# Layer-1 adaLN parts of a hybrid GLA/mLSTM backbone: both 512-column halves of a part summed over the partitions in one step

## The chip, the cores and the metric

The kernel runs on one core of one Trainium2 chip. The metric is the device time of one execution in microseconds (us). Before the change it is 1614.91 us, the median of three runs (1614.43 to 1615.12). One execution was also taken with the hardware profiler; the trace and all rows below are of that one.

The engines are named as the profile names them: PE is TensorE's matmul, PEld its weight load, DVE is VectorE, ACT is ScalarE, POOL is GpSimd, SP is SyncE, which issues nearly all DMAs. Each engine works through its own queue in order.

## What is computed

Two trunk layers, each a token mixer (layer 0 gated linear attention, layer 1 mLSTM) followed by a ConvFFN, over 512 latent tokens and 256 context tokens of width 1024. Each layer is modulated by adaLN: six vectors of 1024 (shift, scale and gate of mixer and FFN) come from a conditioning vector. The context stream has a conditioning vector of its own, and layer 1 needs only the first two of its parts.

```python
for i in range(DEPTH):                      # DEPTH = 2
    need_ctx = i < DEPTH - 1
    mod_l = (silu(c) @ ada_w[i] + ada_b[i])[:, None, :]
    mod_c = silu(c_ctx) @ ada_w[i] + ada_b[i]
    sh1_l, sc1_l, g1_l, sh2_l, sc2_l, g2_l = split(mod_l, 6)
    sh1_c, sc1_c, g1_c, sh2_c, sc2_c, g2_c = split(mod_c, 6)
    h_c = rmsnorm(ctx) * (1 + sc1_c) + sh1_c
    h_l = rmsnorm(x) * (1 + sc1_l) + sh1_l
    o_c, o_l = mixer(h_c, h_l)              # GLA, then mLSTM
    x = x + g1_l * o_l
    h_l = rmsnorm(x) * (1 + sc2_l) + sh2_l
    x = x + g2_l * conv_ffn(h_l)
    if need_ctx:                            # the same for ctx, with g1_c, sc2_c, sh2_c, g2_c
        ...
return rmsnorm(x) * final_g
```

## The kernel before

All activations lie transposed: 128 channels on the partitions, tokens along the row. Large projections are done in a split form: each operand is divided into a rounded high part and a low rest, and `mm3` (lines 384 to 386) issues three matmuls, high x high, high x low, low x high, in the type fp32r. Weights come by DMA into a staging tile (`load_w`, line 362), ACT writes the high part (line 340) and DVE the low part (line 341). Everything else on PE (transposes, state updates of the scans, sums over partitions) is a plain fp32 matmul.

The adaLN vectors of part p and layer l are made by the generator `ada_seq`, one step at a time. A part is 1024 columns of `ada_w`, done in two halves of 512. For each of eight blocks k of 128 input channels one step multiplies the loaded block [128, 512] with a scalar per partition: for k = 0 on ACT (line 555, it starts the accumulator `asum`), else on DVE (line 558, it adds to it). The loads (line 540) run two steps ahead with three buffers. After k = 7 the accumulator must still be summed over the 128 partitions. PE does that with a matrix of ones 32 wide (line 567): four matmuls, each writing another group of 32 partitions of one PSUM tile. ACT copies the result (line 569), the next step turns it by a PE transpose (line 572), and DVE adds the bias into `mod` (line 575 where two streams are done, line 581 where one is). The accumulators share two buffers (`bufs=2`).

With two streams there are two accumulators per half, and the four matmuls are 256 columns wide (two quarters of two accumulators); two transposes follow. With one stream alone there is one accumulator, the four matmuls are 128 wide, and one transpose follows. One stream alone holds for layer 1, parts 2 to 5. A half is ten steps: eight products, one that ends with the sums and the copy, one with the transposes and the add. Part 2 is done in the FFN of layer 0 (`project`, line 1624, one step after a projection), parts 3 to 5 in the four heads of the mLSTM scan.

In the mLSTM, a head's scan alternates with other work through a `Filler`: after each scan step it runs projection steps worth 1.6 us (`FILL1`), and whenever 1.9 us of these have passed it takes one step of the `side` generator, here 15, 19, 18 and 8 steps of `ada_seq` for the four heads. What a generator yields is its cost in us and is taken off what the filler owes. The filler's work is the value projection (tiles `vpsmv`), the gate (`mo`), the keys and queries of the next head (`mk`, `mq`) and the output projection (`po1...`). The scan itself transposes keys (`mkp`, line 1458), ACT scales them (`mktok`, line 1460), PE makes the update (`mu`, line 1465), DVE or ACT adds it to the state (`C`, lines 1469 and 1471), and later `num` (lines 1497 and 1498) gives the outputs. The framework that records the program may place instructions on their engines in another order than they are written.

Of the kernel before, what the change touches and what calls it, by code (L numbers as in the profile page):

```python
# [16 lines left out]
F32 = mybir.dt.float32  # L17
# [3 lines left out]
AF = mybir.ActivationFunctionType  # L21
ALU = mybir.AluOpType
PSUM = bass.MemoryType.PSUM

P = 128
D = 1024
KT = D // P
# [273 lines left out]
class Body:  # L301
# [226 lines left out]
    def ada_seq(self, parts):  # L528

        nc = self.nc
        steps = [(l, part, half, k) for l, part in parts for half in range(2) for k in range(KT)]

        def load(l, part, half, k):
            st = self.pw.tile([P, 512], F32, tag="ada_w", name=f"ast{l}_{part}{half}{k}", bufs=3)
            c = part * D + half * 512
            nc.sync.dma_start(st, self.a['ada_w'][l][k * P:(k + 1) * P, c:c + 512])  # L540
            return st

        ahead = [load(*x) for x in steps[:2]]
        yield 0.0
        for i, (l, part, half, k) in enumerate(steps):
            st, nm = ahead.pop(0), f"{l}_{part}{half}"
            if i + 2 < len(steps):
                ahead.append(load(*steps[i + 2]))

            both = l == 0 or part < 2  # L550
            c = [self.sil[:, k, s:s + 1] for s in range(2 if both else 1)]
            if k == 0:
                acc = [self.pw.tile([P, 512], F32, tag="ada_sum", name=f"asum{s}_{nm}", bufs=2) for s in range(len(c))]
                for s in range(len(c)):
                    nc.scalar.activation(acc[s], st, AF.Copy, scale=c[s])  # L555
            else:
                for s in range(len(c)):
                    nc.vector.scalar_tensor_tensor(acc[s], st, c[s], acc[s], op0=ALU.mult, op1=ALU.add)  # L558
            yield 0.0
            if k < KT - 1:  # L560
                continue

            ps = self.ada_tile(f"ada{nm}")
            n = 256 if both else 128
            for j in range(4):
                x = acc[j % 2][:, j // 2 * n:j // 2 * n + n] if both else acc[0][:, j * n:j * n + n]
                nc.tensor.matmul(ps[32 * j:32 * j + 32, 0:n], self.ones, x, start=True, stop=True)
            ev = self.pw.tile([P, 256], F32, tag="adaev", name=f"aev{nm}", bufs=1)
            nc.scalar.copy(ev[:, :n], ps[:, :n])
            yield n / 474  # L570
            for i_ in range(n // P):
                nc.tensor.transpose(ps[:, 256 + i_ * P:256 + (i_ + 1) * P], ev[:, i_ * P:(i_ + 1) * P], self.ident)
            b = part * KT + half * 4
            if both:
                nc.vector.tensor_tensor(
                    self.mod[l][:, b:b + 4, :].rearrange("p (q i) s -> p q i s", i=2),
                    ps[:, 256:512].rearrange("p (i q s x) -> p q i s x", i=2, q=2, x=32)[:, :, :, :, 0],
                    self.adab[l][:, b:b + 4].rearrange("p (q i) -> p q i", i=2).unsqueeze(3).to_broadcast([P, 2, 2, 2]),
                    op=ALU.add)
            else:  # L580
                nc.vector.tensor_tensor(self.mod[l][:, b:b + 4, 0], ps[:, 256:384:32], self.adab[l][:, b:b + 4], op=ALU.add)
            if half and part in (1, 4):
                self.make_A(l, part // 4, 0, KT, 2 if both else 1)
            yield n / 1164

    def ada_step(self, n=1):
        for _ in range(n):
# [1247 lines left out]
```

## Time and profile before

| | us |
|---|---|
| median of three runs (lowest, highest) | 1614.91 (1614.43, 1615.12) |
| the profiled execution | 1615.44 |
| its span, first to last instruction | 1613.4 |
| PE busy | 1594.7 (99%) |
| DVE busy | 1231.5 (76%) |
| ACT busy | 678.9 (42%) |

A matmul's printed duration runs to its modelled end, and the next one starts before that; so the spacing of starts, and not the duration, says how long a matmul holds the queue. A wait is idle time of an engine, put down to the instruction that came last before it ended. Records of line 567 come in twos: each fp32 matmul there stands as two records, so four matmuls are "x8".

### The profile page before, as it was taken

The numbers are of one execution on the slowest core, as the hardware profiler recorded it, in microseconds if no ns is written. First come the engines' busy times: TensorE is split into PE (matmuls) and PEld (weight loads), VectorE is DVE, ScalarE is ACT, GpSimd is POOL, SyncE is SP. The second block draws the span as 40 slices with busy tenths as digits, with TensorE's granted clock in tenths as the row PEclk, the third lists the DMA queues.
The fourth block names the chain that finished last, engine by engine and source line by source line (L and its number), as shares of the span: only waits on it lengthen the run. The fifth ranks groups of instructions, "written<-read, shape, count | busy, mean of one in ns | idle before, by whom it ended". The sixth has DMA issues, their size and how long they took to land. (4 is left out here: it accounts for less than half of the span.)

```text
span 1613.4 us, 23563 instructions
## 1 busy us (share of the span) xinstructions
PE 1594.7 (99%) x9249; PEld 1379.1 (85%) x9249; DVE 1231.5 (76%) x2123; ACT 678.9 (42%) x1149; POOL 68.6 (4%) x128
## 2 busy tenths in 40 slices
PE   7999999999999999999999999999999999999998
PEld 6789898888888888888888988888889888888887
DVE  5866978878985978686755778766778988877875
ACT  5683738435431314131322356545465422323334
POOL 0010101011000000000000020000001000000000
PEclk9999999999999999999999999999999999999999
DMA  8613453432240524251312204433330423223321
GB/s 303 190 47 107 125 152 92 141 89 88 83 124 27 147 76 118 66 169 50 102 53 63 57 27 150 134 119 102 98 118 14 129 89 97 85 81 98 117 79 53
DMA packets 178674, 163.59 MB, mean 101 GB/s; under 512 B 8924, under 2 KB 146788, under 8 KB 178564
## 3 DMA queue, kind: packets, MB, share of 16 engines
q1 hardware_dynamic: 178324, 161.97, 33.4%
q8 instruction: 72, 1.18, 0.3%
q14 instruction: 38, 0.31, 0.1%
q10 hardware_dynamic: 240, 0.13, 0.0%
HBM read 159.98 MB, written 2.10 MB: 100 GB/s over the span
## 5 line engine op out<-in xcount | busy, mean ns | idle before, releaser
L1648 DVE SCALAR_TENSOR_TENSOR acc<-gp,vt_f,acc 128x512 f32<-128x512 f32 x352 | 260.2, 747 | 4.6
L558 DVE SCALAR_TENSOR_TENSOR asum<-ast,sil,asum 128x512 f32<-128x512 f32 x224 | 163.7, 753 | 21.3 <-ACT asum L555 11.3
L384 PE MATMUL fd<-ahil,wh_d 128*128 128x512 f32 (+1 forms) x376 | 142.0, 378 | 0.3 <-DVE xl L629 0.2
L386 PE MATMUL fd<-ahil,wl_d 128*128 128x512 f32 (+1 forms) x376 | 141.7, 378 | 0.0
L385 PE MATMUL fd<-alol,wh_d 128*128 128x512 f32 (+1 forms) x376 | 141.4, 376 | 0.0
L629 DVE SCALAR_TENSOR_TENSOR xl<-fd,mod,xl 128x512 f32<-128x512 f32 (+1 forms) x128 | 90.7, 714 | 55.7 <-PE fd L386 55.4
L384 PE MATMUL fa<-hhi,wh_a 128*128 128x512 f32 x320 | 124.9, 390 | 0.0
L384 PE MATMUL fg<-hhi,wh_g 128*128 128x512 f32 x320 | 124.8, 390 | 0.0
L385 PE MATMUL fg<-hlo,wh_g 128*128 128x512 f32 x320 | 124.6, 389 | 0.0
L386 PE MATMUL fg<-hhi,wl_g 128*128 128x512 f32 x320 | 124.6, 389 | 0.0
L386 PE MATMUL fa<-hhi,wl_a 128*128 128x512 f32 x320 | 124.6, 389 | 0.0
L385 PE MATMUL fa<-hlo,wh_a 128*128 128x512 f32 x320 | 124.5, 389 | 0.0
L1649 ACT ACTIVATE acc<-acc,vt_f 128x256 f32<-128x256 f32 (+1 forms) x66 | 43.1, 653 | 173.1 <-DVE acc L1648 172.9
L340 ACT CAST wh_a<-st_a 128x1024 fp32r<-128x1024 f32 x43 | 45.2, 1052 | 102.3 <-PE fg L385 86.3
L1632 ACT COPY gp<-fg 128x512 f32<-128x512 f32 x40 | 23.3, 582 | 146.1 <-PE fg L386 146.1
L384 PEld LDWEIGHTS fd<-ahil,wh_d 128*128 128x128 f32 x376 | 70.7, 188 | 13.6 <-DVE xl L629 1.1
L386 PEld LDWEIGHTS fd<-ahil,wl_d 128*128 128x128 f32 x376 | 70.6, 188 | 13.0 <-DVE wl_d L341 0.2
L385 PEld LDWEIGHTS fd<-alol,wh_d 128*128 128x128 f32 x376 | 70.7, 188 | 12.4
L341 DVE TENSOR_TENSOR wl_a<-st_a,wh_a 128x1024 fp32r<-128x1024 f32 x43 | 52.5, 1220 | 33.7 <-ACT wh_a L340 33.7
L340 ACT CAST wh_d<-st_d 128x1024 fp32r<-128x1024 f32 x44 | 45.9, 1050 | 75.9 <-PE fd L385 54.2
L386 PEld LDWEIGHTS fa<-hhi,wl_a 128*128 128x128 f32 x320 | 60.1, 188 | 12.6
L386 PEld LDWEIGHTS fg<-hhi,wl_g 128*128 128x128 f32 x320 | 60.1, 188 | 12.6
(1436 smaller groups left out, 4483.0 us busy)
## 6 DMA issues: line engine op xcount, KB each, us to landing
ast<-in_ada_w_dram SPq DMA_DIRECT2D x160, 256.0 KB
st_g<-in_ffn_w_up_dram SPq DMA_DIRECT2D x44, 512.0 KB
st_a<-in_ffn_w_up_dram SPq DMA_DIRECT2D x44, 512.0 KB
st_d<-in_ffn_w_down_dram SPq DMA_DIRECT2D x44, 512.0 KB
ast<-in_ada_w_dram SPq DMA_DIRECT2D x16, 512.0 KB
st_wo<-in_gla_w_out_dram SPq DMA_DIRECT2D x14, 512.0 KB
st_gr<-in_gla_w_in_dram SPq DMA_DIRECT2D x8, 512.0 KB
st_mo<-in_mlstm_w_in_dram SPq DMA_DIRECT2D x8, 512.0 KB
```

The source lines that it names most:

```text
L340: return (nc.scalar.copy(hi, src), (eng or nc.vector).tensor_tensor(lo, src, hi.bitcast(F32), op=ALU.subtract))
L341: (eng or nc.vector).tensor_tensor(lo, src, hi.bitcast(F32), op=ALU.subtract))
L384: nc.tensor.matmul(ps, wl[0], wr[0], start=start, stop=False)
L385: nc.tensor.matmul(ps, wl[0], wr[1], start=False, stop=False)
L386: nc.tensor.matmul(ps, wl[1], wr[0], start=False, stop=stop)
L558: nc.vector.scalar_tensor_tensor(acc[s], st, c[s], acc[s], op0=ALU.mult, op1=ALU.add)
L629: self.nc.vector.scalar_tensor_tensor(xv, ps, gate, xv, op0=ALU.mult, op1=ALU.add)
L1632: nc.scalar.copy(g[:, 1:ROWS + 1, 1:W_GRID + 1], ps[c0].rearrange("p (r w) -> p r w", r=ROWS))
L1648: nc.vector.scalar_tensor_tensor(o, s, tw, o, op0=ALU.mult, op1=ALU.add)
L1649: nc.scalar.activation(acc[:, c0:c0 + n], acc[:, c0:c0 + n], AF.Gelu_apprx_tanh, bias=cb[:, c:c + 1])
```

## The change

In layer 1, parts 2 to 5, the first half now keeps its accumulator and goes through two empty steps in place of the sums and of the transpose. The second half gets another accumulator, and after its last product four matmuls of 256 columns sum both (two quarters of each accumulator), one copy of 256 columns follows, then two transposes and one add for all eight blocks of the part. The number of steps stays ten per half; the costs that they yield are 0 and 0 for a first half, 0.54 and 0.22 for a second half (before 0.27 and 0.11 for each). Parts with two streams do the same as before, with the same order of matmuls.

```diff
             if k == 0:
-                acc = [self.pw.tile([P, 512], F32, tag="ada_sum", name=f"asum{s}_{nm}", bufs=2) for s in range(len(c))]
+                new = [self.pw.tile([P, 512], F32, tag="ada_sum", name=f"asum{s}_{nm}", bufs=2) for s in range(len(c))]
                 for s in range(len(c)):
-                    nc.scalar.activation(acc[s], st, AF.Copy, scale=c[s])
+                    nc.scalar.activation(new[s], st, AF.Copy, scale=c[s])
+                acc = new if both or not half else acc + new
             else:
                 for s in range(len(c)):
-                    nc.vector.scalar_tensor_tensor(acc[s], st, c[s], acc[s], op0=ALU.mult, op1=ALU.add)
+                    nc.vector.scalar_tensor_tensor(acc[s - len(c)], st, c[s], acc[s - len(c)], op0=ALU.mult, op1=ALU.add)
             yield 0.0
             if k < KT - 1:
                 continue
+            if not (both or half):
+
+                yield 0.0
+                yield 0.0
+                continue
 
             ps = self.ada_tile(f"ada{nm}")
-            n = 256 if both else 128
             for j in range(4):
-                x = acc[j % 2][:, j // 2 * n:j // 2 * n + n] if both else acc[0][:, j * n:j * n + n]
-                nc.tensor.matmul(ps[32 * j:32 * j + 32, 0:n], self.ones, x, start=True, stop=True)
+                q, i_ = (j // 2, j % 2) if both else (j % 2, j // 2)
+                nc.tensor.matmul(ps[32 * j:32 * j + 32, 0:256], self.ones, acc[i_][:, q * 256:q * 256 + 256],
+                                 start=True, stop=True)
             ev = self.pw.tile([P, 256], F32, tag="adaev", name=f"aev{nm}", bufs=1)
-            nc.scalar.copy(ev[:, :n], ps[:, :n])
-            yield n / 474
-            for i_ in range(n // P):
+            nc.scalar.copy(ev, ps[:, :256])
+            yield 0.54
+            for i_ in range(2):
                 nc.tensor.transpose(ps[:, 256 + i_ * P:256 + (i_ + 1) * P], ev[:, i_ * P:(i_ + 1) * P], self.ident)
...
             else:
-                nc.vector.tensor_tensor(self.mod[l][:, b:b + 4, 0], ps[:, 256:384:32], self.adab[l][:, b:b + 4], op=ALU.add)
+                b = part * KT
+                nc.vector.tensor_tensor(
+                    self.mod[l][:, b:b + KT, 0].rearrange("p (q i) -> p q i", i=2),
+                    ps[:, 256:512].rearrange("p (i q x) -> p q i x", i=2, x=32)[:, :, :, 0],
+                    self.adab[l][:, b:b + KT].rearrange("p (q i) -> p q i", i=2), op=ALU.add)
...
-            yield n / 1164
+            yield 0.22
```

In the changed code the products are lines 555 and 559, the sums line 572, the copy line 575, the transposes line 578; everything behind is ten lines further on.

PE in the FFN of layer 0, at the first half of part 2 (`fg` is the gate projection, `ada_20` the PSUM tile of part 2, half 0). Before:

```order
L386 MATMUL fg_7394<-hhi_3904,wl_g_7385 128x512
L567 MATMUL ada_20_7419<-asum_1_20_6924,ones 32x128 x4
L384 MATMUL fg_7426<-chi_3906,wh_g_7384 128x256
L385 MATMUL fg_7426<-clo_3907,wh_g_7384 128x256
L386 MATMUL fg_7426<-chi_3906,wl_g_7385 128x256
```

The changed kernel at the same place:

```order
L386 MATMUL fg_7394<-hhi_3904,wl_g_7385 128x512
L384 MATMUL fg_7419<-chi_3906,wh_g_7384 128x256
L385 MATMUL fg_7419<-clo_3907,wh_g_7384 128x256
L386 MATMUL fg_7419<-chi_3906,wl_g_7385 128x256
L384 MATMUL fg_7419<-chi_3906,wh_g_7384 128x256
```

The four matmuls of 128 columns are gone from here; at the second half of part 2, 386 rows further on, the changed kernel has these:

```order
L385 MATMUL fa_7954<-hlo_3905,wh_a_7881 128x512
L386 MATMUL fa_7954<-hhi_3904,wl_a_7882 128x512
L572 MATMUL ada_21_7979<-asum_1_20_6924,ones 32x256 x2
L572 MATMUL ada_21_7979<-asum_1_21_7488,ones 32x256 x2
L384 MATMUL fa_7986<-chi_3906,wh_a_7881 128x256
L385 MATMUL fa_7986<-clo_3907,wh_a_7881 128x256
```

Both accumulators, of half 0 (`asum_1_20`) and of half 1 (`asum_1_21`), are read at that one place.

ACT at the first product of part 4 (`asum_1_40`; `aev_30` and `aev_31` are the copies of part 3, `mktok` scaled keys of the scan). Before, in the first head of the mLSTM:

```order
L1460 ACTIVATE mktok_9715<-mkp_9713,mcol 128x128
L895 COPY mvt_9461<-vpsmv_9694 128x256
L340 CAST wh_mk_9876<-st_mk_9874 128x1024
L1460 ACTIVATE mktok_9747<-mkp_9745,mcol 128x128
L569 COPY aev_30_9764<-ada_30_9759 128x128
L555 ACTIVATE asum_1_40_10277<-ast_400_10142,sil 128x512
L1460 ACTIVATE mktok_9771<-mkp_9769,mcol 128x128
L340 CAST wh_mq_10000<-st_mq_9998 128x1024
```

The changed kernel, in the second head:

```order
L1470 ACTIVATE mktok_10167<-mkp_10165,mcol 128x128
L1455 ACTIVATE Wt_10088<-Wt_10088 128x512
L1479 COPY C_10171<-mu_10169 128x257
L905 COPY mvt_10047<-vpsmv_10149 128x256
L555 ACTIVATE asum_1_40_10261<-ast_400_10125,sil 128x512
L575 COPY aev_31_10191<-ada_31_10186 128x256
L1470 ACTIVATE mktok_10195<-mkp_10193,mcol 128x128
L1470 ACTIVATE mktok_10219<-mkp_10217,mcol 128x128
L905 COPY mvt_10047<-vpsmv_10201 128x256
```

The product of part 4 has moved from the first head's scan to the second's. It stands in front of the copy of part 3, where before it stood behind that of part 3's first half.

SP from the second part of a head's value weights (`st_mv`) on, in the mLSTM. Before:

```order
L362 DMA st_mv_10072<-in_mlstm_w_in_dram 128x4x256
L540 DMA ast_403_10307<-in_ada_w_dram 128x512
L540 DMA ast_404_10337<-in_ada_w_dram 128x512
L540 DMA ast_405_10382<-in_ada_w_dram 128x512
L540 DMA ast_406_10402<-in_ada_w_dram 128x512
L540 DMA ast_407_10425<-in_ada_w_dram 128x512
L362 DMA st_mo_10368<-in_mlstm_w_in_dram 128x8x128
L540 DMA ast_410_10455<-in_ada_w_dram 128x512
```

The changed kernel:

```order
L362 DMA st_mv_10055<-in_mlstm_w_in_dram 128x4x256
L362 DMA st_mo_10352<-in_mlstm_w_in_dram 128x8x128
L362 DMA st_mo_10413<-in_mlstm_w_in_dram 128x8x128
L362 DMA st_wo_10490<-in_mlstm_w_out_dram 128x1024
L362 DMA st_wo_10496<-in_mlstm_w_out_dram 128x1024
L540 DMA ast_403_10291<-in_ada_w_dram 128x512
```

The loads of part 4 (`ast_403` and on) now stand behind the weights `st_mo` and `st_wo`; before, five of them stood ahead of the first `st_mo`. Between the last `st_wo` and the next head's key weights (`st_mk`) there are eleven loads of `ada_w` now, and eight before.

## Rows read from the trace of the kernel before

**Rows 1.** The page: the span, and busy time (share, instructions) of PE and DVE.

```profile
span 1613.4 us, 23563 instructions
...
PE 1594.7 (99%) x9249; PEld 1379.1 (85%) x9249; DVE 1231.5 (76%) x2123; ACT 678.9 (42%) x1149; POOL 68.6 (4%) x128
```

**Rows 2.** Busy time by engine from 1050 to 1100 us, then granted clock, DMA share, GB/s.

```profile
1050.00:1100.00 50.00, 50.00 (x295) 43.21 (x294) 33.98 (x75) 21.33 (x45) 0.74 (x2) 1.00 0.42 127
```

**Rows 3.** Waits of PE, 940 to 1232 us: total, times, longest.

```profile
PE wib L1425 <- DVE mstk L1339: 0.9, 1, 0.9
PE vpsmv L386 <- POOL hlo L341: 0.3, 1, 0.3
PE po134A L384 <- DVE xl L629: 0.3, 1, 0.3
```

**Rows 4.** Groups of tile ada, 760 to 1230 us: duration ns min/median/max, first and last start.

```profile
L567 PE MATMUL ada<-asum,ones x64: 272/284/298, 767.5 to 1213.0; 128*32 128x128 f32 x64
L569 ACT COPY aev<-ada x8: 243/265/273, 768.0 to 1213.3; 128x128 f32<-128x128 f32 x8
...
L572 PE MATMUL ada<-ident,aev x8: 270/271/272, 770.8 to 1217.8; 128*128 128x128 f32 x8
L581 DVE TENSOR_TENSOR mod<-ada,vt_v x8: 151/155/165, 771.2 to 1219.3; 128x4 f32<-128x4 f32 x8
```

**Rows 5.** Timeline of PE at part 2, first half: start, duration, instruction.

```profile
767.14 0.39 PE L386 MATMUL fg<-hhi,wl_g 128*128 128x512 f32 x1
767.46 0.43 PE L567 MATMUL ada<-asum,ones 128*32 128x128 f32 x8
767.81 0.39 PE L384 MATMUL fg<-chi,wh_g 128*128 128x256 f32 x1
768.04 0.28 PE L385 MATMUL fg<-clo,wh_g 128*128 128x256 f32 x1
```

**Rows 6.** Timeline of PE at a half with two streams (layer 1, part 0).

```profile
521.03 0.39 PE L386 MATMUL fg<-hhi,wl_g 128*128 128x512 f32 x1
...
522.39 0.39 PE L386 MATMUL fg<-hhi,wl_g 128*128 128x512 f32 x1
522.71 0.64 PE L567 MATMUL ada<-asum,ones 128*32 128x256 f32 x8
523.28 0.39 PE L384 MATMUL fg<-chi,wh_g 128*128 128x256 f32 x1
523.51 0.28 PE L385 MATMUL fg<-clo,wh_g 128*128 128x256 f32 x1
```

**Rows 7.** Timeline of PE at the transposes: two together, then one.

```profile
526.12 0.28 PE L386 MATMUL fg<-chi,wl_g 128*128 128x256 f32 x1
526.24 0.38 PE L572 MATMUL ada<-ident,aev 128*128 128x128 f32 x2
526.38 0.47 PE L384 MATMUL fa<-hhi,wh_a 128*128 128x512 f32 x1
526.69 0.39 PE L385 MATMUL fa<-hlo,wh_a 128*128 128x512 f32 x1
...
770.65 0.28 PE L386 MATMUL fg<-chi,wl_g 128*128 128x256 f32 x1
770.78 0.27 PE L572 MATMUL ada<-ident,aev 128*128 128x128 f32 x1
770.80 0.48 PE L384 MATMUL fa<-hhi,wh_a 128*128 128x512 f32 x1
771.12 0.40 PE L385 MATMUL fa<-hlo,wh_a 128*128 128x512 f32 x1
```

**Rows 8.** Waits of ACT, whole span: line 555 on the sums.

```profile
ACT asum L555 <- PE ada L567: 5.8, 4, 1.7
```

**Rows 9.** SP's queue at the key weights of head 2; tile wh_mk's first use.

```profile
1067.16 0.38 SPq L362 DMA_DIRECT2D st_mk<-in_mlstm_w_in_dram  x1
...
L384 PE MATMUL mk<-hhi,wh_mk x8: 389/389/395, 1099.6 to 1104.4; 128*128 128x512 f32 x8
```

More of the change, by code (lines that the diff above doesn't have):

```diff
@@ L561, in ada_seq @@
                 continue
+            if not (both or half):
+                yield 0.0
+                yield 0.0
+                continue
             ps = self.ada_tile(f"ada{nm}")
-            n = 256 if both else 128
             for j in range(4):
-                x = acc[j % 2][:, j // 2 * n:j // 2 * n + n] if both else acc[0][:, j * n:j * n + n]
-                nc.tensor.matmul(ps[32 * j:32 * j + 32, 0:n], self.ones, x, start=True, stop=True)
+                q, i_ = (j // 2, j % 2) if both else (j % 2, j // 2)
+                nc.tensor.matmul(ps[32 * j:32 * j + 32, 0:256], self.ones, acc[i_][:, q * 256:q * 256 + 256],
+                                 start=True, stop=True)
             ev = self.pw.tile([P, 256], F32, tag="adaev", name=f"aev{nm}", bufs=1)
-            nc.scalar.copy(ev[:, :n], ps[:, :n])
-            yield n / 474
-            for i_ in range(n // P):
+            nc.scalar.copy(ev, ps[:, :256])
+            yield 0.54
+            for i_ in range(2):
                 nc.tensor.transpose(ps[:, 256 + i_ * P:256 + (i_ + 1) * P], ev[:, i_ * P:(i_ + 1) * P], self.ident)
-            b = part * KT + half * 4
             if both:
+                b = part * KT + half * 4
                 nc.vector.tensor_tensor(
```

## The prediction

> **What bounds the kernel now.** I read the page first. TensorE (PE) is busy 1594.7 us of a span of 1613.4 us, VectorE 1231.5 us [rows 1]. The stretch 1050 to 1100 shows PE busy for all of its 50 us at a granted clock of 1.00, the upper of its two levels (2.4 GHz), with VectorE at 33.98 us and ScalarE at 21.33 us [rows 2]. So a microsecond that leaves TensorE's queue leaves the span, and work that leaves VectorE or ScalarE buys nothing by itself. Next I asked who PE waits for between 940 and 1232, where the change moves other work: three waits only, 0.9, 0.3 and 0.3 us [rows 3]; hardly a stall is left to be removed. Then I asked which instructions the changed lines own in layer 1: 64 records of the sums over partitions, 8 transposes, 8 copies on ScalarE and 8 adds on VectorE [rows 4]. These are eight halves, for parts 2 to 5 with two halves each.
>
> The sum uses spacing rather than the durations printed for matmuls, because these overlap. From 521.03 to 522.39 there are six steps of 512-column matmuls, 1.36 us: 0.227 each [rows 6]. A step of 256 columns is 0.12, from 526.12 to 526.24 [rows 7]. What an insertion costs is the time from the start of the matmul ahead of it to the start of the second one behind it, less those two steps. The second one is taken because the first one behind an insertion is itself stretched: in both groups, its successor starts 0.23 us after it instead of 0.12 [rows 5, 6].
>
> **The change part by part.** *The sum over partitions.* Now a half is four matmuls of 128 columns (eight records). From 767.14 to 768.04 is 0.90 us; without it 0.227 + 0.12 = 0.347, so it costs 0.55 us [rows 5]. After the change a part is four matmuls of 256 columns. The same program already runs these for the parts with two streams: from 522.39 to 523.51 is 1.12 us, less 0.347 is 0.77 us [rows 6]. Twice the columns cost 0.22 us more, not twice as much. Each part saves 2 x 0.55 - 0.77 = 0.33 us.
>
> *The transposes.* Their number stays 8, but two come together. One alone: 770.65 to 771.12 is 0.47, less 0.347, so 0.12. Two together: 526.12 to 526.69 is 0.57, less 0.347, so 0.22 [rows 7]. A part saves 2 x 0.12 - 0.22 = 0.02 us.
>
> *Together:* 4 x (0.33 + 0.02) = 1.40 us of PE's queue. Bounds: some of the halves stand next to other plain-fp32 matmuls, where the stretch on both sides may be paid anyway. If it always is, only the time from the group's start to the next start counts: 0.35 for 128 columns [rows 5], 0.57 for 256 [rows 6], so 4 x (2 x 0.35 - 0.57 + 0.02) = 0.6 us. At the other end, if a group of the first half takes all its cost away and the second half's becomes no dearer: 4 x (0.55 + 0.12) = 2.7 us. I take 1.40, since both shapes were measured in the same surroundings (a 512-column matmul ahead and 256-column ones behind), where neither bound holds.
>
> The Trainium skill, page "TensorEngine Tiling (Array Packing)", section "Instruction Overhead", says that each matmul carries an overhead of about 60 cycles. By that alone the 16 matmuls that go away would be worth, as an estimate at 2.4 GHz, 16 x 25 ns = 0.4 us, and the time would be 1614.5. The trace disagrees: the group of four with 128 columns costs 0.55 us and that with 256 columns 0.77, so more than 60 cycles per matmul is fixed.
>
> *Copies and adds.* ScalarE loses eight copies of 0.265 us and gets four of 256 columns; VectorE loses four of eight adds of 0.155 us [rows 4]. Costed at nothing: VectorE has 16 us free in 50 and ScalarE 28 [rows 2]. If that cover were gone it would still be a gain.
>
> *The accumulators live longer.* Two buffers hold the sums of a stream, and both are now kept until the second half's matmuls have read them. So the first product of the next part (line 555, ScalarE) must wait for those matmuls. This comes up at two places, part 3 to 4 and part 4 to 5; between parts 2 and 3 lies the rest of the FFN of layer 0. By the order, ScalarE has the product of part 4 in front of the copy of part 3, with the products `mktok` of the scan behind both; a late `mktok` would make PE wait at its `mu`. The trace has this same wait where both streams fill both buffers (layer 0): four times, 5.8 us together, 1.7 at the longest [rows 8]. I take nothing: PE's first `mkp` behind the wait stands itself behind the matmuls that end it, and twelve to fifteen value matmuls of 0.12 us (1.4 to 1.8 us) lie between it and the `mu` that needs it. Upper bound: 1.7 us at each of the two places, 3.4 us.
>
> *Moved accumulation.* Seven VectorE products of part 4's first half (and of part 5's) now come one scan later; they need 7 x 0.75 us there, inside the 16 us that VectorE has free [rows 2]. Nothing reads parts 3 to 5 before the norm and the FFN that follow the mLSTM, and the last matmuls of each part stay where they were.
>
> *DMA queue.* On SyncE the loads of `ada_w` that follow a held buffer now come behind the weights of `mo` and `wo`, and the key weights of the next head stand behind eleven such loads instead of eight. Now that load is issued at 1067.16 and PE's first use of it is at 1099.6 [rows 9], 32 us later; three more loads, each paced by a 0.75 us product and what lies between, do not use that up. Cost 0.
>
> *Filler.* The two yields of a first half now count 0, those of a second half 0.54 and 0.22. The total stays, but around a first half some three to six projection matmuls move across a step of the scan. No matmul is added by this; its cost is nothing or a short stall, bounded by the 0.9 us that is PE's longest wait in that stretch [rows 3].
>
> **The sum.** The profiled execution took 1615.44 us (span 1613.4 plus 2.0 around it), 0.5 above the median of 1614.91. The saving does not depend on that offset, so I take it off the median: 1614.91 - 1.40 = 1613.5 us.
>
> **The rivals.** *Slower: the held accumulators.* ScalarE stands at line 555 until PE has done the part's sums, the scan's products come late, and PE waits for them. Price up to 2 x 1.7 us [rows 8]: 1613.5 + 3.4 = 1616.9. It turns slower than before as soon as more than 0.7 us reaches PE at each place. For it: ScalarE works in order, and the order puts that product ahead. Against it: in the whole stretch PE waits for VectorE and GpSimd and never for ScalarE [rows 3]. Chance 0.20, which includes other short stalls from the moved steps; 0.06 that it passes 0.2%.
>
> *Faster than said: the moved steps close gaps.* If the 0.6 us of the last two waits go [rows 3] the result is 1612.9, and with the upper bound of 2.7 us 1612.2. Against it: little is there to be closed. Chance 0.09, of which 0.05 beyond 0.2%.
>
> *The change does not do what it says: the cost goes by columns.* The columns are the same before and after, so 1614.9; with the lower bound 1614.3. Against it: the two shapes measured above. Chance 0.09, the page's rule of 60 cycles with its 1614.5 among it.
>
> **How the numbers follow.** Forecast 0.62, at 1613.5. The range runs from 1612.2 (upper bound of the saving) to 1616.0 (most of the slower rival); about 0.15 is left out. A difference of 0.2%, 3.2 us, is about what a measurement of this kernel can tell from no change. The whole forecast and nearly all of the rivals lie inside it: faster 0.05, same 0.89, slower 0.06.
>
> **What would show it.** In the changed profile the sum line has 32 records fewer in layer 1, all of 256 columns; the group of part 2's second half (near 834) costs 0.77 us by spacing, and the place near 767 shows 512-column and 256-column matmuls without a break. Wrong would be: a wait of PE for `mktok` or `C` from ScalarE behind either of the two groups in heads 1 and 2 of the mLSTM; a wait of PE for the weights of `mk` or `mq`; or a group of 256 columns that costs 1.1 us, which would make the saving nothing.

## The result and the profile after

The changed kernel takes 1617.92 us (median of 20 runs), the kernel before 1614.82 in the same comparison (20 runs): a ratio of 1.0020, 95% interval 1.0015 to 1.0026. It is slower by 3.1 us; the forecast was 1613.5, the range ended at 1616.0. One disturbed execution each of the changed kernel, of its third run and of the run with early loads is left out of all ratios and ranges given here; without it their medians are 1617.79, 1616.78 and 1615.16.

In the profiled execution (1621.78 us) the page shows the saving and the loss side by side. This is its span and the engines' busy time, which answers [rows 1]; line numbers have moved (sums now L572, copy L575, transposes L578, adds L588, `hps` L849, `mkp` L1468, `mktok` L1470, `C` L1481):

```profile
span 1620.0 us, 23500 instructions
...
PE 1597.1 (99%) x9217; PEld 1381.0 (85%) x9217; DVE 1231.7 (76%) x2119; ACT 675.5 (42%) x1143; POOL 68.1 (4%) x128
```

PE has 32 records fewer, as said, and yet it is counted busy longer. The groups of tile `ada` from 760 to 1230 us answer [rows 4] (duration ns min/median/max, first and last start):

```profile
L572 PE MATMUL ada<-asum,ones x32: 379/391/404, 834.0 to 1219.3; 128*32 128x256 f32 x32
L578 PE MATMUL ada<-ident,aev x8: 270/271/273, 837.6 to 1224.4; 128*128 128x128 f32 x8
```

PE's waits from 940 to 1232 us (total, times, longest), against [rows 3]:

```profile
PE hps L849 <- ACT mktok L1470: 2.4, 1, 2.4
PE mkp L1468 <- DVE C L1481: 1.7, 1, 1.7
PE wib L1435 <- DVE mstk L1349: 1.0, 1, 1.0
PE vpsmv L386 <- POOL hlo L341: 0.3, 1, 0.3
```

The first two are new; a wait of PE for `mktok` behind the sums is what the prediction had named as a sign of its being wrong. They stand at 1140 and at 1068, in the two heads of the scan in which a held accumulator comes free. Behind each of them stands something that the kernel before shows in no such place. Busy time by engine, then the granted clock, DMA share and GB/s, ahead of the first wait, in it, behind it, and behind the second (against [rows 2]):

```profile
1064.00:1068.00 4.00, 4.00 (x32) 3.80 (x31) 1.53 (x4) 3.49 (x6) 0.00 (x0) 1.00 0.61 188
1068.00:1070.00 2.00, 0.51 (x3) 0.07 (x1) 2.00 (x3) 0.00 (x1) 0.00 (x0) 1.00 0.50 144
1071.50:1074.50 3.00, 3.00 (x8) 2.32 (x8) 2.57 (x5) 0.66 (x2) 0.00 (x0) 0.50 0.55 163
1143.00:1146.00 3.00, 2.96 (x10) 2.47 (x11) 1.81 (x3) 2.12 (x4) 0.00 (x0) 0.50 0.83 241
```

PE is busy behind the waits, but at its lower level, 1.2 GHz; the trace's record of the granted clock gives this level for 3.4 us each time. That is why PE's busy time grew. The matmuls show it in their spacing (timeline of PE: start, duration):

```profile
1070.25 0.33 PE L1468 MATMUL mkp<-ident,kT 128*128 128x128 f32 x1 [1.74 <-DVE C L1481]
...
1072.13 0.63 PE L384 MATMUL mo<-hhi,wh_mo 128*128 128x512 f32 x1
1072.55 0.63 PE L385 MATMUL mo<-hlo,wh_mo 128*128 128x512 f32 x1
...
1075.53 0.39 PE L386 MATMUL mo<-hhi,wl_mo 128*128 128x512 f32 x1
1075.76 0.39 PE L384 MATMUL mo<-hhi,wh_mo 128*128 128x512 f32 x1
```

A step of 512 columns takes 0.42 to 0.43 us there and 0.23 at the end: 3.4 us at half clock cost 1.7. The account of the span closes with that. By the spacing of starts the two waits cost 1.9 and 2.6 us, the two stretches at half clock 2 x 1.7, and 1.4 is taken as saved, as forecast: 1.9 + 2.6 + 3.4 - 1.4 = 6.5; the span grew by 1620.0 - 1613.4 = 6.6. This execution is one of the slowest. The kernel's runs spread from 1615.95 to 1621.78 (the kernel before: 1613.78 to 1616.20), and in three traces the waits and the half clock differ. The half clock is not needed for the loss: in the trace of the second run of the changed kernel (1617.88 us, next to the median) the waits are 1.3 and 1.9 us, no half clock stands behind them, PE is busy 1594.0, and the span is still 1615.9 - 1613.4 = 2.5 us longer.

**What is late.** First products of a half (line 555) on ScalarE stood at 1012.0, 1055.2, 1085.6 and 1128.1 in the trace of before, for the halves of parts 4 and 5: 30 to 43 us apart (ScalarE's timeline: start, duration, instruction):

```profile
1012.02 0.73 ACT L555 ACTIVATE asum<-ast,sil 128x512 f32<-128x512 f32 x1
...
1055.19 0.72 ACT L555 ACTIVATE asum<-ast,sil 128x512 f32<-128x512 f32 x1
...
1085.57 0.72 ACT L555 ACTIVATE asum<-ast,sil 128x512 f32<-128x512 f32 x1
...
1128.10 0.71 ACT L555 ACTIVATE asum<-ast,sil 128x512 f32<-128x512 f32 x1
```

Here is the same for the changed kernel (in brackets the idle time ahead and its releaser):

```profile
1054.73 0.72 ACT L555 ACTIVATE asum<-ast,sil 128x512 f32<-128x512 f32 x1 [0.19 <-PE ada L572]
...
1064.30 0.72 ACT L555 ACTIVATE asum<-ast,sil 128x512 f32<-128x512 f32 x1 [0.91 <-DMA ast<-in_ada_w_dram]
...
1130.51 0.72 ACT L555 ACTIVATE asum<-ast,sil 128x512 f32<-128x512 f32 x1 [2.41 <-PE ada L572]
...
1141.74 0.72 ACT L555 ACTIVATE asum<-ast,sil 128x512 f32<-128x512 f32 x1 [2.62 <-DMA ast<-in_ada_w_dram]
1142.37 0.35 ACT L905 COPY mvt<-vpsmv 128x256 f32<-128x256 f32 x1
1142.62 0.37 ACT L1470 ACTIVATE mktok<-mkp,mcol 128x128 f32<-128x128 f32 x1
```

The accumulators are held until 1054, so the first half of part 4 no longer runs at 1012 but at 1055, and the second half follows 10 us behind it, where there are 43 between these two in the kernel before. Part 5's halves go the same way, 1130.5 and 1141.7 in place of 1085.6 and 1128.1. Sixteen products with their loads now come in a row. SP issues the loads as fast as three buffers come free, and no faster (SP's queue; answers [rows 9]):

```profile
1055.48 13.53 SPq L540 DMA_DIRECT2D ast<-in_ada_w_dram  x11
1069.83 0.38 SPq L362 DMA_DIRECT2D st_mk<-in_mlstm_w_in_dram  x1
```

Eleven loads in 13.5 us, one each 1.2 us. The program however places the products among the scan's steps as if the loads were there. At 1141.74 ScalarE has stood 2.62 us for one load, and the next `mktok` comes behind it; PE's `hps` needs the PSUM buffer that this `mktok` reads. Near 1068 it is VectorE that stands, ahead of two products of the second half, with `wl_mo` (1.22 us) and the state update behind them, for which PE's `mkp` waits:

```profile
1067.12 1.54 DVE L559 SCALAR_TENSOR_TENSOR asum<-ast,sil,asum 128x512 f32<-128x512 f32 x2 [2.00 <-ACT mktok L1470]
```

The profile puts these 2.00 us down to `mktok`, which happened to end just then; the product does not read it. In the trace's semaphore events the load's last event stands at 1067.03, 0.09 us ahead of the product. The same 0.09 us lies between the two in the second and third execution of the changed kernel (1066.37 to 1066.46, 1065.27 to 1065.37). So it is the load that VectorE waited for.

### The profile page after: what moved, and what is told of

Same layout as the page of the kernel before. It is cut to its first block, busy times and chain, and to the rows that moved or that the text cites. A ratio compares the mean times of both kernels' runs of the same rounds, so it can differ in the third digit from the quotient of the medians.

```text
span 1620.0 us, 23500 instructions
## 1 busy us (share of the span) xinstructions
PE 1597.1 (99%) x9217; PEld 1381.0 (85%) x9217; DVE 1231.7 (76%) x2119; ACT 675.5 (42%) x1143; POOL 68.1 (4%) x128
```

## Experiments

Ratios are to the kernel before in the same comparison, with 95% intervals. Theory A is what was just told: loads that come late and in a bunch make ScalarE and VectorE stand in front of the scan's work. B is that the moved yields of the filler do it, C that the wide sums do.

**Accumulators of their own.** Part 4 gets two accumulators in a tile that is idle then, so nothing is held; the control makes the same edit to the kernel before.

```diff
...
+                if l == 1 and part == 4:
+                    if not half:
+                        self.ada_x = self.pc.tile([P, 4, 512], F32, tag="xc", name="ada_x", bufs=1)
+                    new = [self.ada_x[:, half, :]]
...
```

> The changed kernel, but part 4 of layer 1 gets accumulators of its own (a tile that lies idle in the mLSTM), so that its first product waits for no sums of part 3, and part 5 uses the buffers that part 3 has left. Theory A (the held accumulators push the next part's loads and products together behind the sums, and products that wait for a late load block ScalarE and VectorE ahead of the scan's own work): the two stalls of PE near 1068 and 1140 us go, with the two stretches at half clock behind them, and the saving of the merged sums is left: about 1613.4 us. Theory B (the moved filler steps, that is the yields of 0 and of 0.54 and 0.22, put the stalls there): the yields are the same, so about 1618. Theory C (the wider sums, copy and add themselves hold PE up): about 1618.

> The kernel before, with the same separate accumulators for part 4: it had no hold to lose, so theories A, B and C all expect 1614.8 us, within 0.7. If it is faster by over 1 us, the separate buffers do something else than theory A says.

The first took 1616.41, ratio 1.0009 (1.0001 to 1.0018), the control 1618.86, ratio 1.0022 (1.0013 to 1.0031). The first is what A wants in part: the wait at 1140 is gone. But that at 1068 stays with 1.2 us and a new one of 1.1 us (`wic`, 1046) comes up, so its 1616.41 fits neither A's 1613.4 nor the 1618 of B and C. The control was not neutral: all theories expected 1614.8. Without the wait for a buffer the framework placed part 4's products further ahead, in front of the work that starts a head's scan: waits of 1.7 and 0.6 us from 1046 on, with 3.4 us of half clock behind them. VectorE did not wait there, it was busy with these products. So a held accumulator is not the only way to bring such a wait about; a product that stands too early in an in-order queue does it as well. For the same reason the pair does not isolate what holding costs.

**The moved yields alone**, in the kernel before:

```diff
-            yield n / 474
+            yield 0.54 if both else 0.54 * half
...
-            yield n / 1164
+            yield 0.22 if both else 0.22 * half
```

> The kernel before, each half summed by itself, but with the yields of the change (0 and 0 for a first half, 0.54 and 0.22 for a second one, in the parts with one stream). Theory A: the filler's steps move, nothing is held: 1614.8 us within 0.7, no PE wait above 1 us between 1010 and 1230. Theory B: the stalls come with the moved steps: about 1618 to 1619.

1615.56, ratio 1.0003 (0.9994 to 1.0012), and no wait of PE beyond those of [rows 3] and one of 0.2. B falls as the cause of the 3 us. It may hold a small part of them: by the starts of the same matmuls this trace loses 0.6 us between 1125 and 1165.

**The change for part 2 alone**, where no other part waits for its accumulators. The other parts keep the old code:

```diff
-                acc = new if both or not half else acc + new
+                acc = new if both or not half or part != 2 else acc + new
...
-            if not (both or half):
+            if not (both or half) and part == 2:
...
+            n = 256 if both or part == 2 else 128
```

> The change for part 2 alone (in the FFN, where no scan runs beside it); parts 3 to 5 as before. Theory A and B: no stall, a quarter of the saving: 1614.5 us (0.35 below before), and by spacing the merged group at the second half of part 2 costs 0.77 us while the one near 767 is gone. Theory C (the wider sums hold PE up): a stall of PE at that group, 1615.5 or more.

1614.65, ratio 0.9998 (0.9989 to 1.0007). The time alone can't tell 0.35 from nothing. The trace can: the start of the same matmul, against the trace of before, is 0.19 us earlier from 400 to 750 and 0.54 earlier from 850 to 900, a gain of 0.35. The price of the sums was right, and the wide sums brought no wait at this place.

**Held accumulators, narrow sums.** The changed kernel, its sums at the end of the second half as eight of 128 columns:

```diff
-            for j in range(4):
+            for j in range(4 if both else 8):
...
+                i_, q = j // 4, j % 4
+                nc.tensor.matmul(ps[32 * q:32 * q + 32, i_ * P:i_ * P + P], self.ones, acc[i_][:, q * P:q * P + P],
...
```

> The changed kernel with everything moved as the change moves it (both halves' accumulators held, two empty steps, one copy, two transposes and one addition at the end of the second half), but the sums themselves as in the kernel before: eight of 128 columns instead of four of 256. The before kernel ran at 1615.1 in the last comparison, the changed one at 1617.9. Theory A (the late first load of a half stands in front of the scan's work on ScalarE and VectorE, because the first product of a half waits for the sums that free its accumulator): the two long waits of TensorE near 1068 and 1140 are there again, with the half clock behind them, and the time is the changed kernel's plus the saving that is undone, four times 0.35: 1618 to 1620. Theory C (the wider sums themselves bring the loss): no long waits, 1614.5 to 1615.5.

1615.29, ratio 1.0004 (0.9995 to 1.0013): neither A's number nor its two long waits. This looked like C. But the framework had also placed six VectorE instructions otherwise: an accumulation of `asum` stood ahead of the scan's update of `C` behind the sums, where the changed kernel has it behind. Two kernels took these two differences apart, beside the changed kernel itself. One has wide sums in the sequence 2, 3, 0, 1, which gives VectorE nearly the order of the narrow run. The other writes each wide sum as two narrow ones, which leaves VectorE's and ScalarE's orders as they are in the changed kernel.

```diff
-            for j in range(4):
+            for j in (range(4) if both else (2, 3, 0, 1)):
```

```diff
+                w = P if not both and j < 4 else 256
+                for o in range(0, 256, w):
+                    nc.tensor.matmul(ps[32 * j:32 * j + 32, o:o + w], self.ones, acc[i_][:, q * 256 + o:q * 256 + o + w],
...
```

> The changed kernel with the four sums of a part issued in another order, those of the second half's accumulator first. Instructions, widths, loads and held accumulators are the same; what differs is where the framework puts six of VectorE's instructions in the mLSTM: an accumulation now stands ahead of the scan's state update behind the sums, as in the run with held accumulators and narrow sums, instead of behind it. Theory D (the loss is decided by that order: the accumulations pace the loads, and with the state updates ahead of them the loads come later than the places at which ScalarE and VectorE are told to wait for them): the waits of TensorE near 1068 and 1140 go and the time is 1614.5 to 1615.5, about 2.5 below the changed kernel. Theory C (wide sums together with held accumulators bring the loss, whatever the order): the waits stay, 1617.5 to 1618.5.

> The changed kernel with each wide sum of a one-stream part written as two of 128 columns, eight instructions in place of four; VectorE's and ScalarE's orders stay those of the changed kernel, word for word. Theory D (the order decides): the waits of TensorE near 1068 and 1140 are there and the time is that of the changed kernel, 1617 to 1619. Theory C (the wide sums do it): no long waits, 1614.5 to 1615.5, as in the run with held accumulators and narrow sums. For the price of the sums: if what a group costs goes by its columns plus one fixed part for each interruption of the projection, these eight cost the 0.77 of four wide ones; if each instruction has its fixed part, 1.1.

> The changed kernel itself once more, on the same chip as the three others of this batch, so that they can be compared with it and not with the kernel before alone. Every theory expects 1617 to 1618.5, with the two long waits of TensorE near 1068 and 1140 in most executions.

They took 1617.54 (ratio 1.0020, 1.0011 to 1.0029), 1617.87 (1.0019, 1.0010 to 1.0028) and 1618.14 (1.0023, 1.0013 to 1.0034). So C falls, narrow sums are as slow as wide ones; but the order of those six instructions does not decide alone either. The narrow run was then repeated beside the changed kernel on one chip:

> The run with held accumulators and narrow sums once more, now beside the changed kernel on one chip. Theory D (small differences in VectorE's order decide whether the late loads reach TensorE): 1615 to 1616 again, at least 1.5 below the changed kernel, no wait of TensorE over 0.8 near 1068 and none near 1140. Theory G (the difference was the chip's): 1617 to 1618.5 like the changed kernel, with the two waits.

> The changed kernel on the same chip as the three others. Theory D: 1617 to 1618.5 again. Theory G: what the run with narrow sums gives, within 0.7.

1615.97 (1.0005, 0.9996 to 1.0014) and 1616.78 (1.0015, 1.0006 to 1.0024): 0.8 us apart, less than the 1.5 expected, and with intervals that overlap; nor was the wait near 1140 gone, as expected. Neither of the two theories of these runs holds. What all these kernels have in common is seen in PE's waits between 1040 and 1160, first the repeated narrow run, then the narrow sums in the changed kernel's order, then the changed kernel's second and third run:

```profile
PE hps L851 <- ACT mktok L1472: 1.0, 1, 1.0
PE mkp L1470 <- DVE C L1483: 0.3, 1, 0.3
```

```profile
PE hps L851 <- ACT mktok L1472: 1.8, 2, 1.5
PE mkp L1470 <- DVE C L1483: 1.4, 1, 1.4
```

```profile
PE hps L849 <- ACT mktok L1470: 1.9, 1, 1.9
PE mkp L1468 <- DVE C L1481: 1.3, 1, 1.3
```

```profile
PE hps L849 <- ACT mktok L1470: 2.1, 1, 2.1
PE mkp L1468 <- DVE C L1481: 1.7, 1, 1.7
```

They are the same two waits in all, of different length. With the sequence 2, 3, 0, 1 they are 1.1 and 1.1, in the first narrow run 0.2 and 0.9. Wherever the accumulators of parts 3 and 4 are held, ScalarE stands for loads between 1040 and 1150, 2.2 to 3.6 us in all. In the changed kernel's first trace:

```profile
ACT asum L555 <- DMA ast<-in_ada_w_dram: 3.5, 2, 2.6
```

The kernel before and the version with parts 2 and 5 alone have no such wait there. But what decides how much of it reaches PE is not shown: the run with the sequence 2, 3, 0, 1 has 2.2 us of it and takes 1617.54, the repeated narrow run has 2.6 and takes 1615.97. VectorE's waits for loads as a sum tell even less; the kernel before has more of them than the changed one's 3.6 in the same stretch, and PE feels none:

```profile
DVE asum L558 <- DMA ast<-in_ada_w_dram: 4.0, 7, 1.4
```

So it must be the place of a wait, ahead of work that PE needs next; this is argued from the chains told here. One of them is seen on VectorE in the second run of the changed kernel, in front of the state update:

```profile
1066.46 1.54 DVE L559 SCALAR_TENSOR_TENSOR asum<-ast,sil,asum 128x512 f32<-128x512 f32 x2 [1.53 <-DMA ast<-in_ada_w_dram]
1067.92 1.22 DVE L341 TENSOR_TENSOR wl_mo<-st_mo,wh_mo 128x1024 fp32r<-128x1024 f32 x1
1069.05 0.48 DVE L1481 SCALAR_TENSOR_TENSOR C<-C,dec,mu 128x257 f32<-128x257 f32 x1
```

**Loads issued earlier.** The changed kernel with four more load buffers and a look-ahead of six steps for most of parts 3 to 5:

```diff
...
-            if i + 2 < len(steps):
-                ahead.append(load(*steps[i + 2]))
+            while at < min(len(steps), i + (7 if deep and 12 <= i < 36 else 3)):
+                ahead.append(load(*steps[at]))
+                at += 1
...
```

> The changed kernel with four more load buffers for parts 3 to 5, in a tile that is idle at that time, and loads issued six steps ahead instead of two; the accumulators are held as in the changed kernel. Theory A in its form that the loads come late (bunched behind the sums, the products wait for them): neither ScalarE nor VectorE waits for a load near 1068 and 1140, the long waits of TensorE and the half clock go, and the time is 1613 to 1614.5, below both kernels. Rival K (the wait for the accumulator alone does it, whenever the loads come): the waits stay, 1617 to 1618.5. Rival L (earlier loads collide with the weights' loads on SP's queue): a wait for a weight tile appears near 1050 to 1150, 1615 to 1618.

1615.64, ratio 1.0002 (0.9993 to 1.0011). The accumulators are held as long as in the changed kernel, and the two long waits are gone: PE's longest behind 1040 is 0.3 us, VectorE's for loads fell from 3.6 us to 1.2 between 1040 and 1150. Rival K falls with that: an accumulator can be held and the two waits be gone. The wait for a weight tile that rival L expects is 0.2 us, on ScalarE. But the framework moved the products as well, ScalarE's first ones of the second halves from 1064.3 and 1141.7 to 1059.2 and 1132.6, and VectorE's order differs. So the run does not tell earlier loads from this other order. It does not reach the 1613 to 1614.5 that was expected. One first product, whose load goes through an old buffer, still stands 3.1 us on ScalarE; no long wait of PE follows, but by the starts of the same matmuls some 1.1 us, the sums' own cost taken out, is lost between 1125 and 1160 in small pieces.

**The first product on GpSimd** in place of ScalarE:

```diff
-                    nc.scalar.activation(new[s], st, AF.Copy, scale=c[s])
+                    if both:
+                        nc.scalar.activation(new[s], st, AF.Copy, scale=c[s])
+                    else:
+                        nc.gpsimd.tensor_scalar(new[s], st, c[s], None, op0=ALU.mult)
```

> The changed kernel with the first product of each one-stream half on GpSimd instead of ScalarE; loads, accumulators and sums stay. Theory A, for the wait near 1140 (ScalarE stands at that product 2.6 us for its load, in front of the copies on which the scan waits): ScalarE's wait for the load and TensorE's wait of 2.4 us there go, with the half clock behind it (1.7): 1613.4 to 1616, at least 2 below the changed kernel's 1617.9; the wait near 1068, in which VectorE stands in front of the scan's state, may stay. Rival H (it is VectorE's accumulations, which wait for the same loads, that hold the scan at both places): both waits stay and the time is 1617 to 1619.

1622.59, ratio 1.0047 (1.0034 to 1.0059; five runs), the slowest of all and outside what either theory gave. At the place for which it was made it did what A says: ScalarE waits for no load there, and PE's wait for `mktok` is gone, with 1.2 us for VectorE's `C` in its place. But the product is slower on GpSimd (1.58 us median against 0.72), and one at 986.8 came after a wait of 1.8 for its load and took 2.54. The framework had also placed four accumulations ahead of `mstk`, with which the first head starts; two of them stood 1.2 and 1.6 us for loads on VectorE, and `mstk` came late, at 996.7 (994.4 in the changed kernel). PE's waits, 940 to 1232:

```profile
PE wib L1438 <- DVE mstk L1352: 3.7, 1, 3.7
PE mkp L1471 <- DVE C L1484: 1.9, 1, 1.9
PE hps L852 <- DVE C L1484: 1.2, 1, 1.2
```

**A wait made on purpose.** The kernel before, with ten (then twenty) copies on VectorE ahead of one state update of head 1:

```diff
+                for _ in range(10 if (h, d, s) == (1, 1, 2) else 0):
+                    nc.vector.tensor_copy(C[d][nx], C[d][p])
```

> The kernel before with ten copies of 128 x 257 on VectorE (each bounded by the 0.48 us of the state's update) ahead of one update of the state in the second head's scan; the copies write what the update then overwrites, so nothing else changes, neither loads nor sums. It measures what a wait of TensorE costs here. Theory M (a wait of about 2 us is followed by 3.4 us of half clock, which costs another 1.7): one wait of TensorE of 1 to 4 us on VectorE near 1065 to 1080, half clock behind it, and a time above the kernel before by that wait plus about 1.7: 1618 to 1620. Rival N (the half clock in the changed kernel has another cause): the wait alone, clock at full level, 1616 to 1618.

> The kernel before with twenty copies of 0.33 us on VectorE ahead of one state update in the second head's scan, 6.6 us in place of the 3.3 that left no wait of TensorE. About half should reach TensorE: a wait of 1.5 to 4 us near 1065 to 1075. Theory M (a wait of about 2 us can be followed by 3.4 us of half clock): in most executions 1.7 us more than the wait, 1618 to 1620, and a spread of 3 us or more between executions. Rival N (the half clock has another cause): the wait alone and the spread of the kernel before, 2.5 us.

1614.65 (ratio 1.0001, 0.9992 to 1.0009) and 1616.14 (1.0005, 0.9996 to 1.0013). Ten copies, some 3 us of VectorE, brought no wait of PE beyond [rows 3]; twenty brought one of 0.5 us. The question that they were made for, what the half clock adds to a wait of 2 us, they could not answer, since no such wait arose. They show something else: in the kernel before, 3 us more of VectorE's time at this place, with the accumulations and state updates placed around it, reach PE with nothing.

**Parts 2 and 5 alone**, run in two comparisons. These are the parts whose accumulators no later part waits for:

```diff
...
-            if not (both or half):
+            if not (both or half) and part in (2, 5):
...
```

> The change for parts 2 and 5 alone, whose held accumulators no later part waits for; parts 3 and 4 as in the kernel before. VectorE, ScalarE and SP keep their order of the kernel before between 1000 and 1150. If the loss comes only from the held accumulators of parts 3 and 4 and the moved order behind them, nothing is lost here and two parts save 0.35 each: before (1614.9) minus 0.7, 1614.0 to 1614.4, which would be below both kernels. If part 5's own moved steps cost (the earlier runs were 0.3 later at its second sums), 1614.4 to 1614.9.

> The change for parts 2 and 5 alone once more: two parts save 0.35 each and no product waits for a held accumulator, so 0.3 to 0.8 below the kernel before, whose median is about 1614.9: 1614.1 to 1614.6. If the first result was chance: within 0.2 of the kernel before.

1614.43, ratio 0.9995 (0.9986 to 1.0003), and 1613.43, ratio 0.9991 (0.9982 to 1.0000). It is the fastest of all versions and below both kernels by its medians, though the first interval holds 1 and the second ends there. By the starts of the same matmuls 0.4 us is gained from 700 us to the end in the second comparison, 0.46 in the first, where 0.7 was expected. Part 2 gave 0.35 in both, part 5 0.38 and 0.36; some 0.25 is lost between 900 and 1030, where the engines' orders are those of the kernel before, and the trace of the kernel before with ten copies loses 0.18 in that stretch too. The rest of the difference of medians in the second comparison lies in the start of the execution: its trace lacks the half clock near 20 us that the trace of before has. SP's queue shows why nothing is lost, in the second run:

```profile
1054.52 8.76 SPq L540 DMA_DIRECT2D ast<-in_ada_w_dram  x8
1065.55 0.38 SPq L362 DMA_DIRECT2D st_mk<-in_mlstm_w_in_dram  x1
```

Eight loads in a row, as in the kernel before; ScalarE waits for none of them, and PE has no wait in these two heads.

## Why the prediction was wrong

- **The sum over partitions was right in size, and its cause was not quite what it was taken for.** The group at 834 costs what was forecast, 0.77 us: 833.70 to 834.82, less 0.347.

```profile
833.70 0.39 PE L386 MATMUL fa<-hhi,wl_a 128*128 128x512 f32 x1
834.02 0.64 PE L572 MATMUL ada<-asum,ones 128*32 128x256 f32 x8
834.59 0.39 PE L384 MATMUL fa<-chi,wh_a 128*128 128x256 f32 x1
834.82 0.28 PE L385 MATMUL fa<-clo,wh_a 128*128 128x256 f32 x1
```

  With held accumulators and eight narrow sums (the run that was repeated) the same place reads:

```profile
832.02 0.39 PE L386 MATMUL fa<-hhi,wl_a 128*128 128x512 f32 x1
832.34 0.64 PE L576 MATMUL ada<-asum,ones 128*32 128x128 f32 x16
832.91 0.38 PE L384 MATMUL fa<-chi,wh_a 128*128 128x256 f32 x1
833.13 0.28 PE L385 MATMUL fa<-clo,wh_a 128*128 128x256 f32 x1
```

  1.11 - 0.347 = 0.76: twice the instructions, the same columns, the same cost (0.79 in the other run with eight narrow sums). So the 0.33 us that does not go by columns (0.55 - 0.22, with 0.22 for each 4 x 128 columns) belongs to the interruption of the projection, not to each matmul as the prediction had it; [rows 5, 6] could not tell these apart, as both have four matmuls. The gain comes from joining two interruptions, and the wide sums add nothing to it. The rule of the Trainium skill that was weighed (page "TensorEngine Tiling (Array Packing)", section "Instruction Overhead", about 60 cycles for each matmul) would make these eight dearer than the four by an estimate of 0.1 us at 2.4 GHz. The traces show no such difference: 0.76 and 0.79 against 0.77.

- **The failed step is "the accumulators live longer: I take nothing", together with "DMA queue, cost 0".** The first followed the wrong wait. It asked how long ScalarE would stand for PE's sums, found 1.7 us and that PE would not feel it. That wait is there (2.41 us at 1130.51), and PE indeed does not feel it. What was missed is the next link: a buffer held longer delays the first product, this delays every load that is issued as buffers come free, and the *second* half's first product, 10 us on, has no load yet. The second step then looked only at who stands behind the loads on SP (the key weights, with 32 us to spare: right) and not at who stands behind the instructions that wait for the loads on ScalarE and VectorE. Measured in its place: PE waits 1.3 to 1.7 us near 1068 and 1.9 to 2.4 near 1140, in three executions of the changed kernel, against the 1.40 us that the sums were to save in all. That the late loads bring these waits is seen in the traces; how long the waits get in a given order stays open.
- **"Seven products, 7 x 0.75 us, inside the 16 us that VectorE has free" counted busy time where order and landing count.** Some 3 us of copies fit in there without any loss to PE, as the made wait showed; two products that wait 1.5 to 2 us for a load, ahead of 1.22 us of `wl_mo`, did not.
- **The slower rival had nearly the right sum (1616.9) by the wrong mechanism.** Its price, two waits of ScalarE's for the sums, is not what PE pays. Its chance of 0.20 rested on [rows 3], in which PE never waits for ScalarE; that was a fact of the old spacing of the products, not of the engine.
- **The half clock was no term at all.** At waits as short as those of [rows 3] the kernel before shows none between 940 and 1232 us. It made the profiled execution slow, not the median one.
- No run shows a cost of the copies and adds. The 0.02 us of a part's transposes is too small for any run to tell. The filler's steps cost 0.6 us at the most in the trace with the yields alone, inside the bound of 0.9.
- The prediction took 0.2% (3.2 us) for the least that a measurement tells from none. The interval of the result is 0.9 us to either side, so its 3.1 us are well told from none.

## What to carry to other kernels

Before a buffer is held longer, follow the whole ring: what its next user loads, how fast those loads can be issued from their own buffers, and which instructions then stand in order behind the ones that wait for them. Free time of an engine does not show that; the distance between a load's issue and its use in the order does. Merging work that interrupts a stream of matmuls pays per interruption, so merge where nobody waits for the buffers, as in parts 2 and 5 here (0.35 and some 0.37 us).

## What the hardware showed unexpectedly

Behind some waits of PE, but not behind all of the same length, the granted clock fell to its lower level for 3.4 us, though PE was busy again. In the first profile of the changed kernel it did so behind both. In the second run (1.3 and 1.9 us) it did so behind neither, and in the third the same two waits, 1.7 and 2.1 us, were followed by the full clock too. The first of these:

```profile
1066.00:1068.50 2.50, 0.79 (x5) 0.32 (x4) 2.46 (x5) 0.28 (x1) 0.00 (x0) 1.00 0.50 159
1068.50:1072.00 3.50, 3.50 (x16) 2.75 (x17) 3.37 (x6) 1.49 (x3) 0.00 (x0) 1.00 0.67 194
```

The spans of the two executions are 1620.0 and 1614.9. 3.4 of these 5.1 us are the two stretches at half clock, and some 1.5 is one more at the start, near 20 us into the span, which the trace of before has too and seven of the kept traces lack, that of the third run among them. In the run with GpSimd a wait of 3.7 us was followed by 6.8 us of half clock. What decides whether it falls is left open here. Each 3.4 us of it cost 1.7, about as much as the wait itself. The executions of the versions in which PE waits for more than 1 us in these heads spread by 3 to 6 us, the kernel before by 2.3 to 3.2; how much of that is the half clock was not measured.
